# A residual stream turned by VectorE in place of TensorE, and weight sums kept split: one planned fp32 layer on one core

## The chip, the cores and the metric

One core of a Trainium2 chip runs the whole layer. The metric is the device time of the run in microseconds (us). TensorE (PE) multiplies, VectorE (DVE) and ScalarE (ACT) do elementwise work, SyncE (SP) issues nearly all transfers between DRAM and on-chip memory, and 16 DMA engines carry them out. Each engine takes its own instructions in the order in which they were emitted, and waits where an operand or a buffer is not ready.

## The reference

The layer has 1024 tokens of width D = 1024 and an FFN of width FF = 3072, all float32:

```python
h = rms_norm(x, norm1_w)
q, k, v, g_ret, x_lru, y_lru, gate_ret, gate_lru = split(h @ w_in)
# A: 4 heads of chunked retention with decay, rotary, group norm, swish gate, @ w_ret_o
# B: causal conv (4), block-diagonal gates, linear recurrence, GeLU branch, @ w_lru_o
x1 = x + (sigmoid(gate_ret) * A + sigmoid(gate_lru) * B) @ w_out
h2 = rms_norm(x1, norm2_w)
g, u = split(h2 @ ffn_w_up)
x2 = x1 + (gelu(causal_conv(g, 3)) * u) @ ffn_w_down
out = rms_norm(x2, norm_f_w)
rms_norm(y, w) = y * rsqrt(mean(y * y, -1) + 1e-6) * w
```

## The kernel before, in words

**Products.** Operands of a product are float32, split in two parts (hi, a cast on ACT, L772; lo = source − hi on DVE, L773), and multiplied in three passes (hi·hi, lo·hi, hi·lo). A job of `mm_fast` makes 256 output columns for all 1024 tokens by the seven products of the Winograd form of Strassen's method: `prod` issues 12 matmuls of 128x512 each (L899), 84 for a job. The weight side needs sums of blocks, S1 to S4 (DVE, L817 to L824), the activation side T1 to T4. The third part of a group is called `wl`, `wrr` or `wsr` where it is lo of a weight, `h…`, `b…` and `t…` are activations, `g` a bank of PSUM.

**Stages.** Times of the profiled execution: values of the heads first (to 95 us); 20 jobs on w_in, with the retention heads and the recurrent blocks as side work between their matmuls (to about 597); 4 jobs each on w_ret_o and w_lru_o (to about 800); 4 jobs on w_out, `out_job(n)`, which make x1 (to about 880); 24 FFN-up jobs (to about 1338); 12 FFN-down jobs in three groups (to 1566); and a tail.

**Order.** The Python code records every operation with its buffers, and a planner (`Prog`) orders them by a table of costs (DMA landing, engine time), with a seed and a jitter for its search. What stands under `within(slack, side)` may be placed later than its place in the code by some slack; `side` work on PE fits between the main matmuls. Any change of operations or of a constant gives a new order everywhere.

**x1 in the kernel before.** A pair n of out_job makes channel blocks 2n and 2n+1: `x1q` holds x by channel (128 channels x 1024 tokens for each block), and L1620 adds the product to it. For n < 3 `turn2` then turns it to token order on PE (128x128 transposes against the identity `cst`, L1680, into a bank `a`), ACT copies the bank to `x1k` (L1686), SP stores x1k to x1_d (by token; `x_d` in the profile), and ACT squares x1k with a sum over channels (L1692) into `nst`. L1642 multiplies x1q by norm2_w in place, `h2_steps` (L1596 to L1605) makes the T sums. For n = 3 the turns come after the jobs, and the scaled values go to a buffer of their own, `x1w` (L1645). The reciprocal root for every token goes to DRAM and comes back on all partitions as `rowt` (L1083); the outputs of FFN up are multiplied by it (L1415). FFN down reads x1_d by token, adds the product (L1813), squares (L1818), takes the root (L1822), multiplies by norm_f_w in place (L1827), scales (L1837 on ACT, L1839 on DVE) and stores (L1840).

**Weight sums ahead of time.** `presum` (L1024 to L1038) makes S1 to S4 for four units of w_out (w0 to w3) and two of w_up (u0, u1), stores them in DRAM (`ss_d`), and their jobs load them (`wr<-ss_d`) and split them. The first presum starts when job 8 of w_in is done, and one follows every second job.

**Retention heads.** Each head's output is turned (L1392), stored to `ot_d`, gathered again as `oc`, and multiplied into its buffers by eight DVE steps (L1406). The convolution of the recurrent branch is a row of DVE steps (L1260).

Of the kernel before, what the change touches and what calls it, by code (L numbers as in the profile page):

```python
# [263 lines left out]
class Prog:  # L264
# [59 lines left out]
    def cost(self, o, how, n, outs, ins, args, kw):  # L324
# [321 lines left out]
    SEED, JITTER, ROUNDS, STALL, URGE = 6, 400.0, 7, 150.0, 6000.0  # L646
# [11 lines left out]
    def emit(self, engines, make, behind):  # L658
        at, sent = {}, []
        for o in self.order:  # L660
# [34 lines left out]
UNS = 1  # L695
# [11 lines left out]
TSLACK = 8000.0  # L707
TEARLY = 6000.0
RELOAD = 0
RNORM = 0  # L710
X1K = 1
HALVES = 0
LATE2 = 2
SQSLACK = 40000.0
PRE = (0, 0, 4, 2)
PRE_AT = 8
PRE_STEP = 2
# [14 lines left out]
def record(prog, fx):  # L732
# [3 lines left out]
    row_d, og_d, u_d, y_d, sg_d, t1_d, x1_d, td_d, to_d, ff_d, rot_d, ss_d, v_d, kt_d, ot_d = (  # L736
        fx[n + "_d"] for n in ("row", "og", "u", "y", "sg", "t1", "x1", "td", "to", "ff", "rot", "ss", "v", "kt", "ot"))
# [38 lines left out]
    def blocks(jb):  # L776
# [17 lines left out]
        def block(nm):  # L794
# [9 lines left out]
            elif jb.pres is not None:  # L804
                if nm == "A22":
                    t = get("wf")
                    SY.dma_start(t, cut(jb.src(1), 1))
                    blk[nm] = *split(t, "w", True), 0
                else:
                    i = int(nm[1])  # L810
                    t = get("wr", FLAT)
                    SY.dma_start(t, jb.pres[i // 2])
                    both(nm, f"S{i + 1}", t, True)
# [210 lines left out]
    def presum(src, dst):  # L1024
# [7 lines left out]
        SY.dma_start(dst[0], s)  # L1032
# [527 lines left out]
    V.memset(rcol, 0.0)  # L1560
    S.activation(st[:, 0:1], st[:, 1:2], AF.Sqrt)
# [22 lines left out]
    x1q, x1w, x1k = {}, [], {}  # L1584
# [26 lines left out]
    def out_job(n):  # L1611
# [3 lines left out]
        def emit(m, h, src, d, sign):  # L1615
            if m not in seen:
                seen.add(m)
                SY.dma_start(q[:, m], xt[:, 2 * n + m].rearrange("h p c -> p h c"))
            t = q[:, m] if h is None else q[:, m, h]
            (V.tensor_add if sign > 0 else V.tensor_sub)(t, t, src)  # L1620
            if n == 3 and HALVES:
                if len(x1w) < 4:
                    x1w.append(get("x1w", QUAD))
                S.activation(x1w[3][:, m, h], t, AF.Copy, scale=pc("norm2_w", 2 * n + m))

        def done(m, d):
            ch = 2 * n + m
            if n == 3 and HALVES:
                if m == 1:
                    next(h2steps)  # L1630
                return
            if UNU:
                if m == 0:
                    x1w.append(get("x1w", QUAD) if n == 3 else q)
                if n < 3:
                    if m == 1:
                        with within(TEARLY, True):
                            for t in range(0, 8, 2):
                                turn2(t, 2 * n, n)
                        with within(TEARLY + 2000.0):  # L1640
                            for i in range(2):
                                S.activation(q[:, i], q[:, i], AF.Copy, scale=pc("norm2_w", 2 * n + i))  # L1642
                            next(h2steps)
                    return
                S.activation(x1w[n][:, m], q[:, m], AF.Copy, scale=pc("norm2_w", ch))  # L1645
                if m == 1:
                    next(h2steps)
            elif UNS:
                hi, lo = scaled_split(q[:, m], pc("norm2_w", ch), "h")
                for h in range(2):  # L1650
                    h2u[f"B{ch // 4 + 1}{h + 1}", ch % 4] = hi[:, h], lo[:, h]

        def post():
            if UNU:
                return None
            if n == 1:
                return turns(0, 4, 0)
            if n == 2:
                return turns(4, 2, 1)

        return Job(pair_src(w_out, n), mop, emit, done, post, fast=n < 4 - STD_W, js=(0, 1, 3, 2), shape=PAIR,
                   pres=pre_of.get(("w", n)))

    def turn(t, ch0, nch, part):
        ps = bank("a")
        for i in range(nch):
            src = x1q[(ch0 + i) // 2][:, (ch0 + i) % 2, t // 4]
            PE.transpose(ps[:, 128 * i:128 * i + 128], src[:, 128 * (t % 4):128 * (t % 4) + 128], ident)
        o = get("x1s")
        S.copy(o[:, :128 * nch], ps[:, :128 * nch])  # L1670
        SY.dma_start(x1_d[128 * t:128 * t + 128, 128 * ch0:128 * ch0 + 128 * nch], o[:, :128 * nch])
        S.activation(ps[:, :128 * nch], ps[:, :128 * nch], AF.Square, accum_out=nst[:, part, t:t + 1])

    def turn2(t, ch0, part):
        ps = bank("a")
        for k in range(2):
            c = 128 * ((t + k) % 4)
            for i in range(2):
                src = x1q[(ch0 + i) // 2][:, (ch0 + i) % 2, t // 4]
                PE.transpose(ps[:, 256 * k + 128 * i:256 * k + 128 * i + 128], src[:, c:c + 128], ident)  # L1680
        if X1K:
            odd = part % 2
            if not odd:
                x1k[t] = get("x1k", PAIR)
            o = x1k[t]
            S.copy(o[:, :, 256 * odd:256 * odd + 256], ps.rearrange("p (k c) -> p k c", k=2))  # L1686
            if odd:
                SY.dma_start(x1_d[128 * t:128 * t + 256, 128 * ch0 - 256:128 * ch0 + 256].rearrange(
                    "(k p) c -> p k c", k=2), o)
                with within(SQSLACK, True):  # L1690
                    for k in range(2):
                        S.activation(o[:, k], o[:, k], AF.Square, accum_out=nst[:, part // 2, t + k:t + k + 1])  # L1692
            return
        o = get("x1s")
        S.copy(o, ps)
        for k in range(2):
            b = slice(256 * k, 256 * k + 256)
            SY.dma_start(x1_d[128 * (t + k):128 * (t + k) + 128, 128 * ch0:128 * ch0 + 256], o[:, b])
            if RELOAD:
                continue  # L1700
            S.activation(ps[:, b], ps[:, b], AF.Square, accum_out=nst[:, part, t + k:t + k + 1])

    def turns(ch0, nch, part):
        for t in range(8):
            turn(t, ch0, nch, part)
            yield 0.9
# [7 lines left out]
    for h in range(2):  # L1714
        for t in range(4 * h, 4 * h + 4, 2 if UNU else 1):
            with within(TSLACK, True):
                if UNU:
                    turn2(t, 6, 3)
                    for i in range(t, t + 2 if RELOAD else t):
                        b = get("xs", FLAT)  # L1720
                        SY.dma_start(b, x1_d[128 * i:128 * i + 128, :])
                        S.activation(b, b, AF.Square, accum_out=nst[:, 0, i:i + 1])
                else:
                    turn(t, 6, 2, 2)
        with within(TSLACK, True):
            a, b, c, e = (nst[:, i, 4 * h:4 * h + 4] for i in range(4))
            v, r = nst[:, 5, 4 * h:4 * h + 4], nst[:, 4, 4 * h:4 * h + 4]
            if not RELOAD:
                V.tensor_add(v, a, b)
            if not RELOAD and not X1K:  # L1730
                V.tensor_add(v, v, c)
            if UNU and not RELOAD and not X1K:
                V.tensor_add(v, v, e)
            V.tensor_scalar(v, a if RELOAD else v, 1.0 / D, EPS, ALU.mult, ALU.add)
            rstd_of(r, v, a)
    rows_of(nst[:, 4, :], True, 1)
    if UNU:
        pass
    elif UNS:
        for k in (0, 1, 4, 5, 2, 3, 6, 7):  # L1740
            rescale(x1q, k, "norm2_w")
        operand(h2, of_quads(x1q), ("B11", "B21", "B22"), False)
    else:
        for h in range(2):
            for k in range(KT):
                t = x1q[k // 2][:, k % 2, h]
# [205 lines left out]
```

## Time and profile before

| | |
|---|---|
| time, median of 3 runs | 1575.1 us (1574.51 to 1575.68) |
| profiled execution, its own time | 1574.89 us |
| its span, first to last instruction | 1573.1 us |
| PE busy | 1563.2 us, 99% |
| DVE busy | 1278.3 us, 81% |
| ACT busy | 883.9 us, 56% |
| granted TensorE clock | 0.999 |
| share of the 16 DMA engines | 56% |

A row of the groups reads: line, engine, operation, output and inputs by name, shape, count | busy time, mean ns of one | idle time of the engine just before them, and what ended it. Matmuls are pipelined, so the durations of neighbours overlap; the distance from start to start is what a matmul takes of the engine's time. A row of the windows gives the stretch and its length, then busy time of PE, its weight loads, DVE, ACT and POOL with the number of instructions that began there, the granted clock, the share of the DMA engines, and GB/s. A row of the DMA issues ends with the median time from issue to landing. A row of the chain of waits gives start, length, and the engine and line that the chain ran through.

### The profile page before, as it was taken

The page shows a single profiled execution, that of the slowest core. Times are in us where ns is not written, and L with a number is a line of the kernel's source. Part 1 is how long each engine was busy: PE and PEld are TensorE (multiplying, and loading weights), DVE is VectorE, ACT ScalarE, POOL GpSimd, SP SyncE. Part 2 cuts the span into 40 slices and gives each one's busy share as a digit, 9 for nine tenths or more (in the row PEclk, how much of TensorE's full clock was granted, in tenths as well). Part 3 has the DMA queues.
Part 4 walks back from the last instruction along what each step waited for, and adds up shares of the span by engine and source line. Part 5 has one row for each costly group of instructions (what it writes and reads, how often), then busy time and mean ns, then how long its engine had stood idle before and what let it go on. Part 6 is the DMA issues. An engine that isn't in the chain of part 4 may idle for free.

```text
span 1573.1 us, 19066 instructions
## 1 busy us (share of the span) xinstructions
PE 1563.2 (99%) x6956; PEld 1295.1 (82%) x6956; DVE 1278.3 (81%) x1712; ACT 883.9 (56%) x1181; POOL 0.2 (0%) x4
## 2 busy tenths in 40 slices
PE   9999999999999999999999999999999999999998
PEld 8888888888878888888888888888888888888886
DVE  5996876988888979978795987788888778977795
ACT  7464567577468568645447854444444445554463
POOL 0000000000000000000000000000000000000000
PEclk9999999999999999999999999999999999999999
DMA  9424354457397579968354522465666335786751
GB/s 333 153 71 150 101 160 147 124 198 261 104 317 261 174 235 349 346 212 336 107 201 151 171 94 70 154 198 185 195 194 219 111 95 194 278 285 249 260 217 67
DMA packets 145150, 303.96 MB, mean 193 GB/s; under 512 B 11168, under 2 KB 60448, under 8 KB 145056
## 3 DMA queue, kind: packets, MB, share of 16 engines
q1 hardware_dynamic: 144624, 302.21, 56.2%
q8 instruction: 55, 0.90, 0.2%
q10 hardware_dynamic: 432, 0.53, 0.1%
q14 instruction: 39, 0.32, 0.1%
HBM read 209.36 MB, written 93.33 MB: 192 GB/s over the span
## 4 chain that ended last, share of the span: by engine, by line
PE 96%; DMA 2%; DVE 1%; ACT 1%; issue 0%; SPq 0%; DVEq 0%; ACTq 0%
PE g L899 84%; PE g L1499 6%; PE a L1273 2%; PE a L1362 1%; PE a L1369 1%; PE a L1361 1%; DMA wgr<-w_gate 1%; PE a L1355 0%; DMA bf<-og_d 0%; PE a L1680 0%; DMA oc<-ot_d 0%; DMA kl<-kt_d 0%; DMA xq<-xt 0%; DVE bf L1017 0%; DVE wrr L773 0%
## 5 line engine op out<-in xcount | busy, mean ns | idle before, releaser
L899 PE MATMUL g<-bh,wh 128*128 128x512 f32 x1728 | 676.2, 391 | 0.0
L899 PEld LDWEIGHTS g<-bh,wh 128*128 128x128 f32 x1728 | 324.5, 188 | 66.2 <-ACT g L920 0.4
L899 PE MATMUL g<-bh,wl 128*128 128x512 f32 x880 | 345.7, 393 | 0.0
L899 PE MATMUL g<-bl,wh 128*128 128x512 f32 x864 | 338.7, 392 | 0.0
L899 PE MATMUL g<-bh,wrr 128*128 128x512 f32 x824 | 321.5, 390 | 0.0
L772 ACT CAST wh<-wr 128x1024 fp32r<-128x1024 f32 (+1 forms) x220 | 198.4, 919 | 71.0 <-DVE wr L824 20.1
L899 PEld LDWEIGHTS g<-bh,wl 128*128 128x128 f32 x880 | 165.2, 188 | 33.9
L899 PEld LDWEIGHTS g<-bl,wh 128*128 128x128 f32 x864 | 162.3, 188 | 33.1
L899 PEld LDWEIGHTS g<-bh,wrr 128*128 128x128 f32 x824 | 154.7, 188 | 32.0
L773 DVE TENSOR_TENSOR wrr<-wr,wh 128x1024 fp32r<-128x1024 f32 (+1 forms) x154 | 152.4, 992 | 35.2 <-ACT wh L772 35.1
L899 PE MATMUL g<-tdr,wh 128*128 128x512 f32 x320 | 124.5, 389 | 0.0
L772 ACT CAST wh<-ws 128x1024 fp32r<-128x1024 f32 x66 | 69.5, 1053 | 81.8 <-DVE ws L818 41.9
L899 PE MATMUL g<-hl,wh 128*128 128x512 f32 x288 | 112.1, 389 | 0.0
L899 PE MATMUL g<-hh,wh 128*128 128x512 f32 x288 | 112.1, 389 | 0.0
L911 DVE TENSOR_TENSOR ub<-ub,g 128x512 f32<-128x512 f32 x72 | 49.4, 686 | 66.1 <-PE g L899 65.9
L773 DVE TENSOR_TENSOR wl<-wr,wh 128x1024 fp32r<-128x1024 f32 x66 | 80.5, 1219 | 8.1 <-ACT wh L772 2.7
L773 DVE TENSOR_TENSOR wl<-ws,wh 128x1024 fp32r<-128x1024 f32 x66 | 80.5, 1220 | 6.0 <-PE g L899 3.9
L906 ACT ACTIVATE ub<-g 128x512 f32<-128x512 f32 x72 | 42.9, 596 | 71.0 <-PE g L899 68.5
L899 PE MATMUL g<-tsr,wh 128*128 128x512 f32 x208 | 81.0, 390 | 0.0
L920 ACT ACTIVATE g<-g 128x512 f32<-128x512 f32 x72 | 41.9, 583 | 55.7 <-PE g L899 55.5
L911 DVE TENSOR_TENSOR ua<-ua,g 128x512 f32<-128x512 f32 x72 | 49.3, 684 | 28.5 <-PE g L899 27.3
L899 PEld LDWEIGHTS g<-tdr,wh 128*128 128x128 f32 x320 | 60.1, 188 | 12.5
(268 smaller groups left out, 2527.0 us busy)
## 6 DMA issues: line engine op xcount, KB each, us to landing
wr<-w_up SPq DMA_DIRECT2D x50, 512.0 KB, 4.5
wr<-w_in SPq DMA_DIRECT2D x48, 512.0 KB, 5.2
dw<-w_dn SPq DMA_DIRECT2D x42, 512.0 KB, 5.7
ff_d<-gc SPq DMA_DIRECT2D x24, 512.0 KB, 3.4
wr<-ff_d SPq DMA_DIRECT2D x24, 512.0 KB, 9.2
td<-td_d SPq DMA_DIRECT2D x24, 512.0 KB, 6.9
x<-x_d SPq DMA_DIRECT2D x24, 512.0 KB, 10.0
td_d<-dw SPq DMA_DIRECT2D x18, 512.0 KB, 6.0
```

Source lines behind the costliest of these rows:

```text
L772: S.copy(hi, src)
L773: V.tensor_sub(lo, src, hi.bitcast(F32))
L899: PE.matmul(ps, (hi, lo)[a][:, c], o[b], start=first and n == 0, stop=n == 11, skip_group_check=True)
L906: S.activation(cut(d[m], h), ps, AF.Copy, scale=scale)
L911: (V.tensor_sub if m else V.tensor_add)(u, u, ps)
L920: S.activation(Y, X, AF.Copy)
L1273: PE.matmul(ps, wg[a][:, g, cs], xs[b][:, k], start=q == 0, stop=q == 5)
L1361: PE.matmul(p2[:, 0:256], q[:, bs], rst[cur], start=True, stop=False)
L1362: PE.matmul(p2[:, 0:256], s, v, start=first, stop=True)
L1369: made.append(PE.matmul(p3[:, 0:256], kd[h][:, bs], v, start=True, stop=True))
L1499: PE.matmul(ps[t], a[i][:, 128 * t:128 * t + 128], b[j], start=k == 0 and i + j == 0, stop=k == KT - 1 and i == 1)
```

## The change

x1 leaves each half of an out job by channel: the half of 128x512 goes to a new DRAM buffer `xb_d`, its square is summed over the channel blocks in `x1s` (a square on ACT, an addition on DVE; the first block of each half squares straight into x1s), and norm2_w multiplies it half by half, in place for n < 3. At the start of FFN up eight fp32 matmuls with `x1s` as the stationary operand and a column of ones sum over the partitions, one result column for 128 tokens. The token order is made during FFN-up jobs 5 to 12: a load of 128 tokens from xb_d (pieces of 512 bytes), one DVE transpose in 32x32 blocks, four stores to x1_d. Since DVE turns only blocks of 32, the channels of x, of the rows of w_in and w_up, the columns of w_out and the norm weights are laid out in another order by the host. The sums of w2, w3, u0 and u1 are split at once and stored as two parts, loaded into `wh` and `wr`, and need no cast and no subtraction later. Presums start after job 4, one at each job. The last norm multiplies into a buffer of its own, `fin`. The planner's cost of an fp32 matmul has a floor, its seed is 4 in place of 6, and options that were off are gone. The 6448 fp32r matmuls are the same.

```diff
-                o.occ, o.lat = 4 * n / 2.4 + 5, 4 * n / 2.4 + 220
+                o.occ, o.lat = max(4 * n / 2.4 + 5, 108), max(4 * n / 2.4, 110) + 220
...
-    SEED, JITTER, ROUNDS, STALL, URGE = 6, 400.0, 7, 150.0, 6000.0
+    SEED, JITTER, ROUNDS, STALL, URGE = 4, 400.0, 7, 150.0, 6000.0
...
+PRE = (0, 0, 4, 2)
+HALVED = ("w2", "w3", "u0", "u1")
...
+TURN0, TURNSLACK = 5, 20000.0
...
-PRE_AT = 8
-PRE_STEP = 2
+PRE_AT = 4
+PRE_STEP = 1
...
-                    SY.dma_start(t, jb.pres[i // 2])
-                    both(nm, f"S{i + 1}", t, True)
+                    p, done = jb.pres
+                    if done:
+                        v, t = get("wh", FLAT, F32R), get("wr", FLAT, F32R)
+                        SY.dma_start(v.bitcast(F32), p[i // 2, 0])
+                        SY.dma_start(t.bitcast(F32), p[i // 2, 1])
+                        for c, n in ((0, nm), (TH, f"S{i + 1}")):
+                            blk[n] = v, t, c
+                    else:
+                        t = get("wr", FLAT)
+                        SY.dma_start(t, p[i // 2, 0])
+                        both(nm, f"S{i + 1}", t, True)
...
+            if halved:
+                hi, lo = split(t, "w", True)
+                SY.dma_start(to[0], hi.bitcast(F32))
+                SY.dma_start(to[1], lo.bitcast(F32))
...
             (V.tensor_add if sign > 0 else V.tensor_sub)(t, t, src)
...
+            with within(TEARLY, True):
+                SY.dma_start(xb_d[k, :, TH * h:TH * h + TH], t)
+                acc = x1s[0][:, h]
+                z = get("x1z") if h in x1s[1:] else acc
+                S.activation(z, t, AF.Square)
+                if h in x1s[1:]:
+                    V.tensor_add(acc, acc, z)
+                x1s.append(h)
+            with within(TEARLY + 2000.0):
+                S.activation(x1w[n][:, m, h], t, AF.Copy, scale=pc("norm2_w", k))
...
-                            for t in range(0, 8, 2):
-                                turn2(t, 2 * n, n)
...
-                PE.transpose(ps[:, 256 * k + 128 * i:256 * k + 128 * i + 128], src[:, c:c + 128], ident)
...
+    def turn(t):
+        a, b = get("x1t", FLAT), get("x1r", FLAT)
+        SY.dma_start(a.rearrange("p (k i) -> p k i", k=KT), xb_d[:, :, P * t:P * t + P].rearrange("k p i -> p k i"))
+        V.transpose(b.view(lambda z: z.rearrange("p (c k j) -> p k c j", c=4, k=KT), FLAT[1]),
+                    a.view(lambda z: z.rearrange("p (k c i) -> p k c i", k=KT, c=4), FLAT[1]))
+        for i in range(4):
+            SY.dma_start(x1_d[P * t:P * t + P, 256 * i:256 * i + 256].rearrange("(c i) r -> i c r", c=4),
+                         b[32 * i:32 * i + 32].rearrange("i (c r) -> i c r", c=4))
...
+        for t in range(8):
+            PE.matmul(ps[:, t:t + 1], x1s[0][:, t // 4, P * (t % 4):P * (t % 4) + P], fx["ones"], start=True, stop=True)
+        V.tensor_scalar(v, ps, 1.0 / D, EPS, ALU.mult, ALU.add)
+        rstd_of(r, v, a)
...
+            if TURN0 <= i < TURN0 + 8:
+                with within(TURNSLACK, True):
+                    turn(i - TURN0)
...
-            V.tensor_mul(cut(d, h), cut(d, h), cut(nf, h))
+            if m not in fin:
+                fin[m] = get("fin", FLAT)
+            V.tensor_mul(cut(fin[m], h), cut(d, h), cut(nf, h))
...
+    perm = ar(D).reshape(4, KT, 32).transpose(1, 0, 2).ravel()
```

Three places of the order. In the changed file the lines are a few higher or lower: the main matmul is L905 there, the cast L770, the subtraction L771, the gathered head's step L1423, the convolution's L1277.

TensorE where FFN up begins (`g` is the PSUM bank of a product, `wh`, `wrr`, `wfr`, `wr` the weights, `a` the bank of the small results). Before:

```order
L899 MATMUL g_7083<-bh_6751,wfr_7110 128x512
L899 MATMUL g_7265<-hh_6869,wh_7217 128x512
L899 MATMUL g_7265<-hl_6880,wh_7217 128x512
L1680 MATMUL a_7206<-cst,x1q_7129 128x128 x3
L1680 MATMUL a_7208<-cst,x1q_7129 128x128 x3
L899 MATMUL g_7265<-hh_6869,wrr_7271 128x512
L899 MATMUL g_7265<-hh_6869,wh_7217 128x512
L899 MATMUL g_7265<-hl_6880,wh_7217 128x512
```

and now:

```order
L905 MATMUL g_7319<-bl_6968,wh_7174 128x512
L905 MATMUL g_7319<-bh_6956,wr_7178 128x512
L905 MATMUL g_7319<-bh_7029,wh_7174 128x512
L1681 MATMUL a_7337<-ones,x1s_6807 128x1 x8
L905 MATMUL g_7319<-bl_7066,wh_7174 128x512
L905 MATMUL g_7319<-bh_7029,wr_7178 128x512
```

The transposes of the last pair stood two matmuls behind the first product of FFN up; no transposes stand there now, and the eight ones matmuls stand 30 main matmuls behind the first of FFN up.

ScalarE during the out jobs. Before:

```order
L1686 COPY x1k_6826<-a_6765 128x2x256
L1686 COPY x1k_6830<-a_6767 128x2x256
L1686 COPY x1k_6844<-a_6833 128x2x256
L1642 ACTIVATE x1q_6552<-x1q_6552,par 128x1024 x2
L1686 COPY x1k_6863<-a_6840 128x2x256
L772 CAST hh_6869<-x1q_6552 128x1024
```

and now, at a later pair:

```order
L1648 ACTIVATE x1z_7101<-x1q_6810 128x512
L1648 ACTIVATE x1z_7115<-x1q_6810 128x512
L926 ACTIVATE g_7126<-g_7088 128x512
L1653 ACTIVATE x1q_6810<-x1q_6810,par 128x512
L770 CAST hh_7141<-x1q_6810 128x1024
L912 ACTIVATE ub_7149<-g_7113 128x512
L770 CAST bh_7154<-ts_6943 128x1024
L1653 ACTIVATE x1q_6810<-x1q_6810,par 128x512
```

The copies of banks are gone; squares stand ahead of the scalings, and each scaling of a half (L1653) stands directly ahead of the cast that makes an operand of it.

VectorE at the end of the second retention head. Before:

```order
L1406 SCALAR_TENSOR_TENSOR ua_2335<-oc_2752,par,ua_2335 128x8x32
L1406 SCALAR_TENSOR_TENSOR ub_2317<-oc_2770,par,ub_2317 128x8x32
L1406 SCALAR_TENSOR_TENSOR ua_2335<-oc_2752,par,ua_2335 128x8x32
L1406 SCALAR_TENSOR_TENSOR ub_2317<-oc_2770,par,ub_2317 128x8x32 x2
L911 TENSOR_TENSOR ub_2749<-ub_2749,g_2702 128x512
L773 TENSOR_TENSOR wl_2867<-wr_2677,wh_2755 128x1024
L773 TENSOR_TENSOR wl_2877<-ws_2773,wh_2794 128x1024
```

and now:

```order
L1423 SCALAR_TENSOR_TENSOR ub_2385<-oc_2871,par,ub_2385 128x8x32
L917 TENSOR_TENSOR ua_2841<-ua_2841,g_2793 128x512
L1423 SCALAR_TENSOR_TENSOR ub_2385<-oc_2871,par,ub_2385 128x8x32
L1423 SCALAR_TENSOR_TENSOR ua_2391<-oc_2854,par,ua_2391 128x8x32
L1423 SCALAR_TENSOR_TENSOR ub_2385<-oc_2871,par,ub_2385 128x8x32
L1277 SCALAR_TENSOR_TENSOR xc_2866<-ub_2537,par,xc_2866 128x1023
L771 TENSOR_TENSOR wl_2952<-ws_2837,wh_2888 128x1024
```

A convolution step now stands between the last scalings of the gathered head and the remainder `wl` that the next product needs; the addition `L917` stands between the scalings and no longer behind them.

More of the change, by code (lines that the diff above doesn't have):

```diff
@@ L694 @@
 STD_LO = 0
-UNS = 1
 LEAD = 3
@@ L735, in record @@
     rst, bst, mv, rs = fx["rst"], fx["bst"], fx["mv"], fx["rs"]
-    row_d, og_d, u_d, y_d, sg_d, t1_d, x1_d, td_d, to_d, ff_d, rot_d, ss_d, v_d, kt_d, ot_d = (
-        fx[n + "_d"] for n in ("row", "og", "u", "y", "sg", "t1", "x1", "td", "to", "ff", "rot", "ss", "v", "kt", "ot"))
+    row_d, og_d, u_d, y_d, sg_d, t1_d, x1_d, xb_d, td_d, to_d, ff_d, rot_d, ss_d, v_d, kt_d, ot_d = (
+        fx[n + "_d"] for n in ("row", "og", "u", "y", "sg", "t1", "x1", "xb", "td", "to", "ff", "rot", "ss", "v", "kt", "ot"))
     x, positions, normf, w_in, w_v, w_ro, w_lo, w_out, w_up, w_dn, w_gate, out, xt = (
@@ L1560, in record @@
     V.memset(rcol, 0.0)
+    V.memset(fx["ones"], 1.0)
     S.activation(st[:, 0:1], st[:, 1:2], AF.Sqrt)
@@ L1583, in record @@
     h2, h2u = {}, {}
-    x1q, x1w, x1k = {}, [], {}
+    x1q, x1w, x1s = {}, [], []
     def h2_steps():
@@ L1615, in emit @@
         def emit(m, h, src, d, sign):
+            k = 2 * n + m
+            if not x1s:
+                x1s.append(get("x1s", PAIR))
+            if not seen:
+                x1w.append(get("x1w", QUAD) if n == 3 else q)
             if m not in seen:
                 seen.add(m)
-                SY.dma_start(q[:, m], xt[:, 2 * n + m].rearrange("h p c -> p h c"))
-            t = q[:, m] if h is None else q[:, m, h]
+                SY.dma_start(q[:, m], xt[:, k].rearrange("h p c -> p h c"))
@@ L1626, in done @@
+            with within(TEARLY + 2000.0):
+                S.activation(x1w[n][:, m, h], t, AF.Copy, scale=pc("norm2_w", k))
         def done(m, d):
-            ch = 2 * n + m
-            if n == 3 and HALVES:
-                if m == 1:
+            if m == 1:
+                with within(TEARLY + 2000.0):
                     next(h2steps)
[L1631 to L1637, printed above, removed]
-                            for t in range(0, 8, 2):
-                                turn2(t, 2 * n, n)
[L1640 to L1661, printed above, removed]
-                   pres=pre_of.get(("w", n)))
[L1664 to L1706, printed above, removed]
+        return Job(pair_src(w_out, n), mop, emit, done, fast=n < 4 - STD_W, js=(0, 1, 3, 2), shape=PAIR,
+                   pres=pre_of.get(("w", n)))
+    def turn(t):
[6 more added lines that the diff above has]
+                         b[32 * i:32 * i + 32].rearrange("i (c r) -> i c r", c=4))
@@ L1713, in record @@
     drain()
[L1714 to L1735, printed above, removed]
-    rows_of(nst[:, 4, :], True, 1)
[L1737 to L1746, printed above, removed]
-                V.scalar_tensor_tensor(t, t, pc("norm2_w", k), cut(row[0], h), ALU.mult, ALU.mult)
-                if k % 2:
-                    put(h2, f"B{k // 4 + 1}{h + 1}", k % 4 // 2, split(x1q[k // 2][:, :, h, :], "h"))
+    with within(TSLACK, True):
+        a, r, v, ps = nst[:, 0, 0:8], nst[:, 4, 0:8], nst[:, 5, 0:8], bank("a")[:, 0:8]
+        for t in range(8):
+            PE.matmul(ps[:, t:t + 1], x1s[0][:, t // 4, P * (t % 4):P * (t % 4) + P], fx["ones"], start=True, stop=True)
+        V.tensor_scalar(v, ps, 1.0 / D, EPS, ALU.mult, ALU.add)
+        rstd_of(r, v, a)
+    rows_of(nst[:, 4, :], True, 1)
     def post_ff(i, gv):
@@ L1768, in down_of @@
         return fetch
-    if not UNU:
-        tsets(h2, of_quads(x1q))
     def emit_row(m, h, src, d, sign):
@@ L1786, in post @@
                 return sums_of(down_of(g), td_d[g], jp)
-        plain = UNS and i < STD_U and not UNU
+        plain = False
         return Job(pair_src(w_up, i), h2u if plain else h2, emit_row if plain else emit_as(),
@@ L1799, in down_job @@
     def down_job(g, t):
-        x1, fin = {}, set()
+        x1, fin = {}, {}
         def fetch(m):
@@ L1834, in done @@
             for c in (m, 1 - m):
-                o, to = cut(d, c), out[rows(t, m), TH * c:TH * c + TH]
+                o, to = cut(fin[m], c), out[rows(t, m), TH * c:TH * c + TH]
                 if c == m:
```

45 lines of the change are left out of this document (23 added, 22 removed).

## The prediction

> **What bounds the kernel now.** I read the page's busy lines first, then its chain that ended last, then busy time stage by stage, then the pieces of the chain around the edited code.
>
> ```profile
> span 1573.1 us, 19066 instructions
> PE 1563.2 (99%) x6956; PEld 1295.1 (82%) x6956; DVE 1278.3 (81%) x1712; ACT 883.9 (56%) x1181; POOL 0.2 (0%) x4
> PE 96%; DMA 2%; DVE 1%; ACT 1%; issue 0%; SPq 0%; DVEq 0%; ACTq 0%
> ```
>
> TensorE is busy 99% of the span and is 96% of the chain, so a change shows only by the TensorE work that it adds or removes, or by a wait that it makes or ends. The stages, with the columns start:end, length, then busy time of PE, its weight loads, DVE and ACT:
>
> ```profile
> 0.00:95.00 95.00, 93.69 (x414) 78.10 (x415) 73.96 (x123) 55.31 (x80) 0.20 (x4) 1.00 0.58 203
> 160.00:280.00 120.00, 120.00 (x541) 99.98 (x540) 92.38 (x144) 79.50 (x107) 0.00 (x0) 1.00 0.44 137
> 280.00:440.00 160.00, 160.00 (x726) 133.63 (x725) 138.02 (x237) 98.96 (x136) 0.00 (x0) 1.00 0.56 183
> 450.00:597.00 147.00, 146.11 (x651) 120.32 (x650) 126.88 (x185) 98.63 (x131) 0.00 (x0) 1.00 0.71 245
> 817.00:885.00 68.00, 67.41 (x328) 55.65 (x327) 49.67 (x56) 46.59 (x68) 0.00 (x0) 1.00 0.49 160
> 885.00:1330.00 445.00, 445.00 (x1964) 368.44 (x1964) 362.92 (x400) 216.05 (x287) 0.00 (x0) 1.00 0.47 151
> ```
>
> PE idles 1.31 us in the first stage, which the change leaves alone, 0.89 us at the last retention heads (450 to 597), 0.59 us where the out jobs end (817 to 885), and nowhere in FFN up. The granted clock is 1.00 throughout.
>
> **The change part by part.**
>
> *The 64 transposes leave TensorE.* The chain has them as pieces (start, us, count); two of the fourteen groups and what ends the stage:
>
> ```profile
> 824.44 0.66 PE a L1680 x6
> 825.10 0.92 PE g L899 x4
> 826.02 0.87 PE a L1680 x8
> ...
> 877.86 0.57 issue
> 878.43 1.23 DVE wrr L773
> ...
> 884.55 0.44 PE a L1680 x4
> 884.99 680.97 PE g L899 x3004
> ```
>
> 0.66/6, 0.87/8 and 0.44/4 all give 0.109 us, so 64 cost 7.0 us of the path; the last row gives a plain matmul's share, 680.97/3004 = 0.2267 us, the ruler for the gaps below. The groups view shows longer durations:
>
> ```profile
> L1680 PE MATMUL a<-cst,x1q 128*128 128x128 f32 x64 | 9.3, 272 | 0.3 <-DVE x1q L1620 0.3
> L1680 PEld LDWEIGHTS a<-cst,x1q 128*128 128x128 f32 x64 | 7.7, 140 | 2.3 <-DVE x1q L1620 0.7
> L1355 PE MATMUL a<-ua,ub 128*128 128x128 f32 x64 | 11.8, 273 | 0.0
> L1355 PEld LDWEIGHTS a<-ua,ub 128*128 128x128 f32 x64 | 11.5, 189 | 2.3
> ```
>
> The 272 ns overlap the neighbour's; the chain's spacing counts. **−7.0 us.** The Trainium skill (TensorE: Matmul & The Clock Gate, Part 4: PE-mode transpose) gives about 275 ns for such a transpose inside a kernel. The 272 ns row agrees as a duration; as a cost on the path the chain's 0.109 us contradicts it, and I go by the chain.
>
> *Eight one-column matmuls come.* An fp32 matmul is two passes (L1355 has 64 for 32 products), so 16 passes, each with its 128x128 weights. No row has one output column. Below, they cannot cost less than nothing, since they add work to TensorE; above, if no weight load is hidden, 16 x 0.189 = 3.0 us. The nearest row is the same fp32 weight form with 128 columns, spaced 0.109 us like the transposes, and their own 140 ns loads fitted in that spacing: 16 x 0.109 = **+1.75 us**. By the Trainium skill (same page, Back-to-back issue gap: up to 64 columns about 25 ns) an estimate is 16 x 0.025 = 0.4 us, and the sum would be 1.35 us lower. No row of this trace tests that.
>
> *The boundary of out and up.* The 0.59 us idle here is two waits, both at the last out pair:
>
> ```profile
> PE a L1273 <- ACT li L1275: 0.7, 1, 0.7
> PE a L1680 <- DVE x1q L1620: 0.3, 1, 0.3
> PE g L899 <- DVE wrr L773: 0.3, 1, 0.3
> ```
>
> The transposes waited for the last residual addition, and the weight remainder stood behind that addition on DVE. In the new order nothing on PE waits for that addition at once: the ones matmuls stand 30 matmuls after the first up matmul, 31 x 0.2267 = 7.0 us, while the square and the addition to x1s that they need end about 6.1 us after it (a sum over the DVE and ACT rows ahead at 0.69, 1.22 and 0.63 us). A margin of 0.9 us; and the weight sums of the first up unit come already split there, without a DVE step. **−0.6 us.** PE takes its instructions in order: if the margin goes, the ones matmuls wait, and all up matmuls behind them are late by as much.
>
> *DVE and ACT in the out stage.* What leaves and what comes:
>
> ```profile
> L1686 ACT COPY x1k<-a 128x512 f32<-128x512 f32 x16 | 9.1, 587 | 12.7 <-PE a L1680 12.7
> L1692 ACT ACTIVATE x1k<-x1k 128x512 f32<-128x512 f32 x16 | 9.9, 631 | 0.2 <-DMA x_d<-x1k 0.2
> L1642 ACT ACTIVATE x1q<-x1q,par 128x1024 f32<-128x1024 f32 x6 | 6.6, 1152 | 0.0
> L1620 DVE TENSOR_TENSOR x1q<-x1q,g 128x512 f32<-128x512 f32 x8 | 5.5, 684 | 5.5 <-PE g L899 5.5
> L773 DVE TENSOR_TENSOR wl<-ws,wh 128x1024 fp32r<-128x1024 f32 x66 | 80.5, 1220 | 6.0 <-PE g L899 3.9
> 1568.91 0.72 ACT ub L1837
> ```
>
> ACT loses 16 x 0.587 + 16 x 0.631 + 8 x 1.152 (six and two more for the last pair) = 28.7 us and gets 16 scalings of half size at 0.72 (the last row, same form) and 16 squares at 0.63 = 21.6: lighter by 7. DVE gets 14 additions x 0.684 = 9.6 us on top of 49.67 of 68, and loses the subtractions of two out units and two up units, 8 x 1.22 = 9.8, part of them here. Both stay far below 68: **0**, hidden by the matmuls. If that cover went, the DVE part would cost 9.6 us at most.
>
> *A new wait.* For the first three pairs the scaling overwrites x1q in place, so ACT's L1653 of the new kernel waits until the store of the same half to xb_d has landed. Stores of this size and of twice it in rows of this trace:
>
> ```profile
> x_d<-x1k SPq DMA_DIRECT2D x8, 512.0 KB, 4.6
> bf<-og_d SPq DMA_DIRECT2D x14, 512.0 KB, 8.2
> v_d<-v SPq DMA_DIRECT2D x16, 256.0 KB, 2.4
> ```
>
> In the new order the tightest scaling comes 17 matmuls = 3.85 us behind its store, with 1.8 us more until PE needs what follows it. At 2.4 us ACT does not wait; queued behind ACT's scaling are the casts of the activations that PE multiplies next. **0**, bounded above by the slowest row, 8.2 us: 8.2 − 3.85 − 1.8 = 2.55 us for each of six channel blocks, 15.3 us.
>
> *Eight VectorE transposes in FFN up, and x1_d by 32 stores.*
>
> ```profile
> L1392 DVE STREAM_TRANSPOSE ox<-ob 128x1024 f32<-128x1024 f32 x8 | 9.9, 1236 | 0.2
> x<-x_d SPq DMA_DIRECT2D x24, 512.0 KB, 10.0
> ```
>
> 8 x 1.24 = 9.9 us into the 82 us that DVE has free between 885 and 1330. Their loads are issued 15 to 44 matmuls (3.4 to 10 us) ahead, so a load of 10.0 us would hold DVE for up to 6.6 us. The first weights split behind any of them are used at least 68 matmuls later, 15.4 us: **0**. x1_d is read only in FFN down. The SP queue is passed by 64 more transfers; in the out stage the engines' DMA share is 0.49.
>
> *Weight sums earlier, and stored split.* Six units' sums (4 additions each, 24 x 0.68 = 16.3 us of DVE) move from 312 to 552 us to about 170 to 335, with the 9.8 us of subtractions of the split ones. DVE has 27.6 us free in 160 to 280 and 22.0 in 280 to 440. So the room suffices by a little: (92.38 + 138.02 x 55/160 + 26.1 less the 2.7 of the one unit that is there now) / 175 = 93%: **0**, with rival B as the price of it going wrong.
>
> *The tail.* Today the last Square is followed by a scaling on ACT, and the root after it starts late:
>
> ```profile
> 1567.24 0.19 ACT L1818 ACTIVATION_READ_ACCUMULATOR a<-ub 128x1 f32 x1
> 1567.34 0.71 ACT L1837 ACTIVATE ua<-ua,nst 128x512 f32<-128x512 f32 x1
> 1567.95 0.28 ACT L1822 ACTIVATE nst<-nst 128x1 f32<-128x1 f32 x1
> ```
>
> In the new order the root stands right behind the Square (0.5 us won) and the last addition behind one more DVE scaling (about 0.35 lost): **−0.15 us**.
>
> *Sum.* 1573.1 − 7.0 + 1.75 − 0.6 − 0.15 = 1567.1 us span. The profiled execution took 1574.89, 1.8 more than its span: 1568.9; the median of the runs is 1575.1, 0.2 above it: **1569.1 us**, 0.4% less. Layout, buffer and planner constants cost nothing of themselves; the order they lead to is what was read.
>
> **The rivals.** A measurement of this kernel tells about 0.2% (3.15 us) from no change.
>
> *B: a new PE wait at the second head's end.* The order puts eight scalings of the gathered head at about 334 us ahead of the remainder wl that PE needs next. Prices, and what DVE did at such a place before:
>
> ```profile
> L1406 DVE SCALAR_TENSOR_TENSOR ua<-oc,par,ua 128x256 f32<-128x256 f32 x16 | 7.7, 480 | 2.2 <-DMA oc<-ot_d 2.1
> L1260 DVE SCALAR_TENSOR_TENSOR xc<-ua,par,xc 128x1023 f32<-128x1023 f32 x4 | 5.1, 1282 | 2.7 <-ACT xc L1256 2.7
> 446.88 0.48 DVE L1406 SCALAR_TENSOR_TENSOR ub<-oc,par,ub 128x256 f32<-128x256 f32 x1 [1.49 <-DMA oc<-ot_d]
> ```
>
> Behind a late oc load stand five scalings, one addition, one convolution step and the subtraction itself: 5 x 0.40 + 0.60 + 1.28 + 1.22, with their starts some 5.6 us, against three matmuls (0.7 us) on PE in the same stretch of the order: 4.9 us, hence 1574.0, no change. For it: the 1.49 us wait for oc above, and the crowded DVE. Against it: at 446.88 the same pile of 7 us made no PE wait, since DVE ran ahead of the order by then.
>
> *G: the small terms all go well.* The 0.89 us at the last heads goes with the sums moved out of there, and the one-column passes cost a share near their column's: 1569.1 − 0.9 − 1.35 = 1566.9. For it: the idle time lies where presums stood. Against it: its largest piece, 0.7, waits for ACT li, which a load precedes.
>
> *C: the in-place scaling waits for its store.* The mechanism above: from a landing of 3.85 + 1.8 = 5.65 us on ACT holds PE, at 8.2 us by 15.3 us in all: 1584.4, slower (slower by 0.2% from some 7.2 us). Against it: stores of 256 KB take 2.4 us.
>
> *D: each transpose costs its whole 272 ns.* Then 64 x 0.272 = 17.4 us leave, 10.4 more: 1558.7. Against it: the chain's rows lie end to end at 0.109.
>
> That the change does not do what it says is excluded by the order: the transposes' rows are gone from PE and nothing but the eight ones rows came.
>
> **How the numbers follow.** Forecast A 0.63, B 0.18, G 0.13, C 0.04, D 0.02. A's own range, from the ends of the one-column passes (0 to 3.0) and stalls of a microsecond either way, is 1566.3 to 1571.4. The range 1565.5 to 1573.0 holds A, G and the half of B with a smaller wait; C, D and the other half, 0.15, are left out. Faster by more than 0.2% means below 1571.9: A but for 0.02 (0.61), G, D and a fifth of B (0.04) = 0.80. Same: the rest of A and B = 0.16. Slower: C = 0.04.
>
> **What would show it.** Right: PE's busy time down by about 5.3 us in 817 to 890, no L1680 group, a group of 16 ones passes spaced about 0.11 us apart, no PE idle at the boundary, the last matmul ending about 6 us earlier. Wrong: in the waits of PE, a row ending in DVE wl or ACT wh near 200, 334 or 446 us (B); ACT idle until DMA xb_d ahead of L1653 (C); ones rows 0.19 us apart; DVE idle until DMA x1t with PE waiting after it.

## The result and the profile after

The changed kernel takes 1567.12 us (median of 6 runs, 1566.76 to 1568.2) against 1575.34 (6 runs, 1574.51 to 1576.17): 0.9948 of the time before, 95% interval 0.9936 to 0.9961, so 8.2 us faster. Its profiled execution took 1568.2 us with a span of 1566.4; a later one (e5) 1567.54 with 1565.7. First the page's span, busy times and chain of the changed kernel:

```profile
span 1566.4 us, 19108 instructions
PE 1556.1 (99%) x6908; PEld 1289.9 (82%) x6908; DVE 1294.6 (83%) x1727; ACT 879.1 (56%) x1158; POOL 0.2 (0%) x4
PE 98%; DMA 1%; DVE 0%; ACT 0%; issue 0%; SPq 0%; ACTq 0%; DVEq 0%
```

TensorE (PE) is still 99% busy, with 7.1 us less to do (1563.2 before); DVE does 16 us more in a shorter span, and it did not matter. The stages, with the columns as before:

```profile
0.00:95.00 95.00, 92.46 (x413) 77.12 (x414) 73.28 (x119) 55.71 (x79) 0.20 (x4) 1.00 0.57 203
160.00:280.00 120.00, 120.00 (x540) 99.94 (x539) 100.44 (x159) 77.26 (x104) 0.00 (x0) 1.00 0.59 199
280.00:440.00 160.00, 160.00 (x725) 133.43 (x725) 140.74 (x240) 103.02 (x142) 0.00 (x0) 1.00 0.58 190
450.00:597.00 147.00, 146.16 (x653) 120.85 (x652) 125.73 (x180) 106.20 (x137) 0.00 (x0) 1.00 0.61 210
817.00:888.00 71.00, 71.00 (x322) 59.03 (x321) 59.23 (x73) 44.83 (x64) 0.00 (x0) 1.00 0.66 244
888.00:1330.00 442.00, 442.00 (x1951) 365.80 (x1950) 365.72 (x395) 207.58 (x265) 0.00 (x0) 1.00 0.53 173
```

From 817 to 888 PE no longer idles at all. At the last heads (450 to 597) it idles 0.84 us, as before (0.89), though at another place. In the first stage, whose work did not change, it idles 2.54 us here; in e5, the same kernel in the same order, 1.35. So a microsecond of difference between two executions comes from the start alone, and a comparison of two single traces is good to about that. What the chain shows where FFN up begins, and the waits of PE in the whole trace:

```profile
875.89 3.17 PE g L905 x14
879.07 1.68 PE a L1681 x16
880.74 9.46 PE g L905 x41
```

```profile
PE g L1516 <- ACT hh L1104: 1.5, 1, 1.5
PE g L1574 <- DVE sc L1571: 1.0, 1, 1.0
PE a L1379 <- DVE state L1390: 0.8, 1, 0.8
```

The 16 passes of the eight ones matmuls cost 1.68 us, 0.105 each. No wait for x1 is left; of the three waits two belong to the start and one (0.8) to a retention head.

Where the time went, by start-to-start distances on PE between 815 and 890 us, less 0.2267 us for every main matmul there: 8.51 us were left before (64 transposes, their switches and waits, beside 293 main matmuls) and 1.87 now (16 passes beside 322). That is −6.64 of the −6.7 us between the two spans. The tail, from the last matmul's start to the end, is 0.25 us shorter; by start-to-start distances the first stage lost 0.3, and the heads kept what they had, give or take.

### The profile page after: what moved, and what is told of

Same layout as the page of the kernel before. It is cut to its first block, busy times and chain, and to the rows that moved or that the text cites. A ratio compares the mean times of both kernels' runs of the same rounds, so it can differ in the third digit from the quotient of the medians.

```text
span 1566.4 us, 19108 instructions
## 1 busy us (share of the span) xinstructions
PE 1556.1 (99%) x6908; PEld 1289.9 (82%) x6908; DVE 1294.6 (83%) x1727; ACT 879.1 (56%) x1158; POOL 0.2 (0%) x4
## 4 chain that ended last, share of the span: by engine, by line
PE 98%; DMA 1%; DVE 0%; ACT 0%; issue 0%; SPq 0%; ACTq 0%; DVEq 0%
PE g L905 87%; PE g L1516 6%; PE a L1290 3%; PE a L1379 1%; PE a L1378 1%; PE a L1386 1%; PE a L1372 0%; DMA xq<-xt 0%; DMA wr<-w_in 0%; DMA to_d<-bf 0%; PE a L1681 0%; ACT a L1752 0%; ACT fin L1773 0%; DVE ua L917 0%; PE g L1521 0%; DVE wrr L771 0%
## 5 line engine op out<-in xcount | busy, mean ns | idle before, releaser
L905 PE MATMUL g<-bh,wh 128*128 128x512 f32 x1728 | 676.2, 391 | 0.0
L905 PEld LDWEIGHTS g<-bh,wh 128*128 128x128 f32 x1728 | 324.4, 188 | 66.8 <-ACT g L926 0.3
L905 PE MATMUL g<-bh,wl 128*128 128x512 f32 x880 | 344.1, 391 | 0.0
L905 PE MATMUL g<-bl,wh 128*128 128x512 f32 x864 | 339.0, 392 | 0.0
L905 PE MATMUL g<-bh,wrr 128*128 128x512 f32 x768 | 299.5, 390 | 0.0
L770 ACT CAST wh<-wr 128x1024 fp32r<-128x1024 f32 (+1 forms) x216 | 195.1, 916 | 75.3 <-PE g L905 21.1
L905 PEld LDWEIGHTS g<-bh,wl 128*128 128x128 f32 x880 | 165.2, 188 | 34.6 <-DVE wl L771 0.7
L905 PEld LDWEIGHTS g<-bl,wh 128*128 128x128 f32 x864 | 162.3, 188 | 33.1
L771 DVE TENSOR_TENSOR wrr<-wr,wh 128x1024 fp32r<-128x1024 f32 (+1 forms) x150 | 147.5, 984 | 33.1 <-ACT wh L770 32.9
L905 PEld LDWEIGHTS g<-bh,wrr 128*128 128x128 f32 x768 | 144.2, 188 | 29.9
L770 ACT CAST wh<-ws 128x1024 fp32r<-128x1024 f32 x70 | 73.7, 1052 | 94.1 <-DVE ws L824 54.6
L905 PE MATMUL g<-tdr,wh 128*128 128x512 f32 x320 | 124.5, 389 | 0.0
L905 PE MATMUL g<-hh,wh 128*128 128x512 f32 x288 | 112.0, 389 | 0.0
L905 PE MATMUL g<-hl,wh 128*128 128x512 f32 x288 | 112.0, 389 | 0.0
L917 DVE TENSOR_TENSOR ub<-ub,g 128x512 f32<-128x512 f32 x72 | 49.3, 685 | 54.7 <-PE g L905 46.5
L771 DVE TENSOR_TENSOR wl<-wr,wh 128x1024 fp32r<-128x1024 f32 x66 | 80.4, 1218 | 12.0 <-PE g L905 6.1
L771 DVE TENSOR_TENSOR wl<-ws,wh 128x1024 fp32r<-128x1024 f32 x66 | 80.5, 1219 | 8.5 <-PE g L905 5.5
L905 PE MATMUL g<-tsr,wh 128*128 128x512 f32 x208 | 81.0, 389 | 0.0
L917 DVE TENSOR_TENSOR ua<-ua,g 128x512 f32<-128x512 f32 x72 | 49.3, 684 | 34.4 <-PE g L905 33.6
L912 ACT ACTIVATE ua<-g 128x512 f32<-128x512 f32 x72 | 43.0, 597 | 60.6 <-PE g L905 56.8
```

What stands on the lines that cost most here:

```text
L770: S.copy(hi, src)
L771: V.tensor_sub(lo, src, hi.bitcast(F32))
L905: PE.matmul(ps, (hi, lo)[a][:, c], o[b], start=first and n == 0, stop=n == 11, skip_group_check=True)
L912: S.activation(cut(d[m], h), ps, AF.Copy, scale=scale)
L917: (V.tensor_sub if m else V.tensor_add)(u, u, ps)
```

## The experiments

All ratios are to the kernel before, run beside it on the same chip. e1 to e4, e5 to e8 and e9 to e12 shared a chip each.

**e1, 64 transposes put back**, of a constant tile, planned with the rest:

```diff
+    def spin(n):
+        for t in range(0, 8, 2):
+            ps = bank("a")
+            for k in range(4):
+                PE.transpose(ps[:, 128 * k:128 * k + 128], ident, ident)
...
             if m == 1:
+                if n < 3:
+                    with within(TEARLY, True):
+                        spin(n)
...
+        spin(3)
         a, r, v, ps = nst[:, 0, 0:8], nst[:, 4, 0:8], nst[:, 5, 0:8], bank("a")[:, 0:8]
```

> The changed kernel (1567.1 us) with 64 transposes of 128x128 put back on TensorE, in the same places of the out jobs but of a constant tile into a bank that nobody reads, so that they bring no ACT copy, no store and no wait for x1. Theory (the gain is the transposes' issue time, 0.109 us each): +7.0 us, 1574.1, so nearly the time of the kernel before. Rival D (a transpose costs its whole 272 ns row): +17.4, 1584.5. Rival plan (the gain comes from a luckier order and fewer waits; the transposes were hidden): within 1.5 us of 1567.1.

Measured: 1576.77 us, 1.0013 (1.0004 to 1.0022), about 10 us above the changed kernel. More than the theory's 7.0, far less than 17.4, and not the time of the changed kernel, as a mere gain of a luckier order would have it. The trace shows why it decides nothing finer: the planner moved the free transposes about (some to 262 us, 25 in a row at 406) and gave a new order with waits of its own, such as these two.

```profile
PE g L905 <- DVE wl L771: 0.6, 1, 0.6
PE a L1290 <- DVE xsl L771: 0.4, 1, 0.4
```

So e7 repeats it with the order held.

**e7, the same 64 transposes in the changed kernel's own order**, emitted after the planning directly ahead of the ones matmuls (`mark` holds the bank of the ones matmuls and the identity, and in e12 also `xb_d`):

```diff
+            if o.eng == "PE" and o.args[0].base is self.mark[0].base and not sent_extra:
+                sent_extra.append(1)
+                for j in range(64):
+                    real.transpose(self.mark[0][:, 128 + 128 * (j % 3):256 + 128 * (j % 3)].ap(), self.mark[1].ap(), self.mark[1].ap())
             inst = at[o.line](getattr(real, o.how), args, kw)
```

> The changed kernel in exactly its own order, with 64 transposes of a constant tile emitted in one row directly ahead of the ones matmuls, after the planning, so that nothing else moves. Theory (0.109 us each): +7.0 us over the changed kernel. Rival D (272 ns each): +17.4. If such a row of small work lowers the granted clock as the 64 passes of one column did (it fell from 1.00 to 0.5 after 3.8 us of them): 3.8 us at 0.109 and then 29 at 0.213, +10 us, and some slow matmuls behind it.

Measured: 1573.48 us, 0.9995 (0.9986 to 1.0004); the changed kernel beside it 1566.61 (e5). The difference is 6.9 us, 0.107 for each. The chain of e7 (L674 are the added transposes, L1687 the ones matmuls):

```profile
877.94 6.99 PE a L674 x64
884.93 1.68 PE a L1687 x16
886.61 676.05 PE g L909 x2981
```

6.99/64 = 0.109 us, to the third digit what the chain of the kernel before had. Rival D is out: a transpose shows as 272 ns in the groups, and its removal saves 109. The row of 7 us did not lower the clock either:

```profile
880.00:884.00 4.00, 4.00 (x39) 4.00 (x37) 2.53 (x3) 0.00 (x0) 0.00 (x0) 1.00 0.08 33
884.00:888.00 4.00, 4.00 (x32) 3.74 (x31) 0.17 (x1) 0.10 (x1) 0.00 (x0) 1.00 0.00 0
```

**e2, the ones matmuls four times over**, all in one row:

```diff
-        for t in range(8):
+        for t in (*range(8),) * 4:
             PE.matmul(ps[:, t:t + 1], x1s[0][:, t // 4, P * (t % 4):P * (t % 4) + P], fx["ones"], start=True, stop=True)
```

> The changed kernel with the eight one-column fp32 matmuls made four times over, 48 more passes. Theory (spaced as in the trace of the changed kernel, 1.68 us for 16): +5.0 us, 1572.1. By the weight loads' own 0.19 us each, none hidden: +9.1, 1576.2. By the issue floor of one column that the skill's page states (25 ns): +1.2, 1568.3.

Measured: 1576.58 us, 1.0013 (1.0004 to 1.0022): about 10 us above the changed kernel for 48 more passes. By the numbers alone the second expectation (9.1, weight loads unhidden) would be taken. The trace says otherwise. The chain, and then the windows (the column ahead of the last two is the granted clock):

```profile
878.47 9.97 PE a L1681 x64
888.43 21.57 PE g L905 x86
```

```profile
879.00:881.00 2.00, 2.00 (x20) 2.00 (x20) 2.00 (x3) 0.90 (x2) 0.00 (x0) 1.00 0.69 259
881.00:885.00 4.00, 4.00 (x26) 4.00 (x25) 2.12 (x2) 0.00 (x0) 0.00 (x0) 0.65 0.02 10
885.00:890.00 5.00, 5.00 (x21) 4.71 (x21) 0.17 (x1) 0.90 (x2) 0.00 (x0) 0.50 0.00 0
890.00:893.00 3.00, 3.00 (x9) 2.33 (x9) 2.33 (x4) 2.13 (x3) 0.00 (x0) 0.60 0.00 0
893.00:900.00 7.00, 7.00 (x32) 5.76 (x31) 4.47 (x12) 3.71 (x6) 0.00 (x0) 1.00 0.09 31
```

The passes start 0.112 us apart for the first 3.8 us, then 0.213 apart, and the clock stands at 0.50; it is back only some 4 us after the row, so that the first plain matmuls are slow too. A wait for weights would be there from the first passes on.

**e8, the same 64 passes in four groups of 16**, with 24 plain matmuls between, in the changed kernel's own order. The sums of those plain matmuls are not used (they repeat the operands of the last main matmul, `last`), and the extra work is 48 passes and 72 matmuls of 504 columns:

```diff
...
+            if o.eng == "PE" and o.args[0].base is self.mark[0].base:
+                for _ in range(3):
+                    at[o.line](getattr(real, o.how), args, kw)
+                sent_extra.append(1)
+                if len(sent_extra) in (2, 4, 6):
+                    for _ in range(24):
+                        real.matmul(self.mark[0][:, 8:512].ap(), last[0][1], last[0][2][:, 0:504], start=True, stop=True, skip_group_check=True)
```

> The changed kernel in its own order, with the eight ones matmuls made four times over as before, but in four groups of 16 passes with 24 plain matmuls of 504 columns between them. Theory (the passes cost 0.112 us, and the second half of them was slow only because a long row of one-column work lowered the granted clock): all 64 passes spaced by 0.11 us, clock 1.00 throughout, 7.2 us for them in all. Rival (the passes themselves get slow after some number of them, or the clock falls by their number and not by the length of the row): spacing 0.21 us in the later groups, and the clock below 1.

```profile
878.34 1.68 PE a L1693 x16
880.02 5.58 PE a L681 x24
885.60 1.68 PE a L1693 x16
887.28 5.55 PE a L681 x24
892.83 1.68 PE a L1693 x16
894.50 5.55 PE a L681 x24
900.05 1.68 PE a L1693 x16
```

```profile
885.00:890.00 5.00, 5.00 (x32) 4.45 (x31) 0.00 (x0) 0.00 (x0) 0.00 (x0) 1.00 0.00 0
890.00:895.00 5.00, 5.00 (x32) 4.46 (x31) 0.00 (x0) 0.00 (x0) 0.00 (x0) 1.00 0.01 3
```

Every group costs 1.68 us, 6.7 in all against 9.97 in one row, and the clock stays at 1.00 (one run, 1589.12 us, which holds the plain matmuls too). So the loss of e2 is the length of the row, not the number of passes. The theory's price for the change's own 16 passes holds.

**e3 and e6, the way of x1 alone**: the weight sums as before.

```diff
-HALVED = ("w2", "w3", "u0", "u1")
+HALVED = ()
-PRE_AT = 4
-PRE_STEP = 1
+PRE_AT = 8
+PRE_STEP = 2
```

> The changed kernel with the weight sums as before: none kept split, first presum after job 8 and one at every second job. What is left is the way of x1. Theory (the sums' change is hidden and worth nothing): 1567.1 within 1.5 us, the scatter of a new order. Rival (the earlier, split sums gave a part of the gain, since the idle time at 440 to 480 us went with them): 1568.6 to 1571, with PE waiting again between 440 and 600 us.

> The kernel with only the way of x1 changed (weight sums as before) once more, beside the changed kernel on one chip. Theory (the sums are worth nothing): within 1.5 us of the changed kernel. Its earlier trace has 1.1 us less of waiting on TensorE than the changed kernel's, so if that holds it is 1 us faster. Rival (the split sums gave a part of the gain): 1.5 us or more slower.

Measured: 1567.54 (0.9957, 0.9944 to 0.9969) and 1567.63 (0.9954, 0.9941 to 0.9966). e5, the changed kernel itself beside e6:

> The changed kernel itself, beside the next ones on the same chip, as their base: ratio 0.9948 to the kernel before, as in its first runs (0.9936 to 0.9961).

gave 1566.61 (0.9949, 0.9935 to 0.9962). The difference of 1.0 us lies inside both intervals, and the spans of e5 and e6 (1565.7 and 1565.4) stand the other way round. The expectation of e6 that the way of x1 alone would be 1 us faster, by its shorter waits, did not hold. The sums bring at most about a microsecond; the way of x1 alone makes the gain.

**e4, e9, e10, e11, the planner's seed.** Each is one of the two kernels with nothing but the seed changed; e4's edit, and the others likewise:

```diff
-    SEED, JITTER, ROUNDS, STALL, URGE = 4, 400.0, 7, 150.0, 6000.0
+    SEED, JITTER, ROUNDS, STALL, URGE = 6, 400.0, 7, 150.0, 6000.0
```

> The changed kernel with the planner's seed of the kernel before (6). Only the order differs. Theory (the seed is worth the idle of PE at a few places, 1 us or so): 1566.1 to 1568.6. Rival (the order of seed 4 was picked and other orders lose several us at a retention head's end): 1570 or more, with a PE wait of 2 us or more in one place.

> The kernel before with the planner's seed of the change (4). Only the order differs. Theory (the change is worth 5.2 us of TensorE's issue time whatever the order; a seed moves the waits by a few us): 1574 to 1579, so that at seed 4 the change is worth 7 to 12 and at seed 6 (e4) 3.5. Rival (seed 4 is the better order for either kernel, and part of the 8.2 us is the seed): 1570 to 1573.

> The kernel before with a third seed (5). Theory: 1574 to 1579, by the waits that its order has. With seeds 4 and 6 it gives a mean over orders of the kernel before.

> The changed kernel with the same third seed. Theory: 1567 to 1571 (between seed 4 and seed 6), and the mean over the three seeds 5 to 6 us below the mean of the kernel before. Rival (the gain is the choice of a lucky order): the means differ by 3 us or less.

| seed | kernel before | changed kernel |
|---|---|---|
| 4 | 1575.68, 1.0003 (0.9994 to 1.0013) | 1566.61, 0.9949 (0.9935 to 0.9962), the change as it is |
| 5 | 1577.58, 1.0018 (1.0008 to 1.0027) | 1571.46, 0.998 (0.9971 to 0.9989) |
| 6 | 1, as it was | 1570.89, 0.9976 (0.9967 to 0.9985) |

The mean of the three ratios is 1.0007 before and 0.9968 after: 0.0039, or 6.1 us. By medians on one chip the change is worth 3.5 us at seed 6 (1574.42 to 1570.89) and 6.1 at seed 5, by the ratios 8.5 at seed 4. The two orders of the changed kernel that were slower lose it mostly ahead of the out jobs, so not by the way of x1: of seed 6's 3.7 us of PE waits behind the start, 3.3 lie there. Seed 6, the longest of its PE waits, and seed 5, its chain at ret_o with a window of it:

```profile
PE g L905 <- ACT ua L912: 1.2, 2, 0.7
PE g L1574 <- DVE sc L1571: 1.0, 1, 1.0
PE g L905 <- DVE ub L917: 0.9, 1, 0.9
PE g L905 <- DVE wl L771: 0.8, 1, 0.8
```

```profile
613.99 1.23 DVE ds L1017
615.22 1.14 DVE li L1306
616.35 0.60 DVE wrr L771
616.96 1.13 DVE li L1308
618.09 1.15 DVE wrr L771
619.28 30.92 PE g L905 x128
620.00:623.00 3.00, 3.00 (x9) 2.31 (x8) 1.60 (x2) 1.55 (x2) 0.00 (x0) 0.50 1.04 392
```

In the second, DVE works off the last recurrent block and two weight remainders; PE goes on until 617.7 us and then stands still for 1.6. Behind that the granted clock is 0.50, and the next matmuls start 0.43 us apart in place of 0.227: the 128 of the last chain row take 1.9 us more than at 0.2267. So the wait cost about 2 us, and the clock about as much again. The kernel before at seed 5 instead waits at the place that the change removes:

```profile
PE a L1680 <- ACT x1k L1686: 1.6, 1, 1.6
PE a L1680 <- DVE x1q L1620: 0.8, 1, 0.8
```

So the rival of e11 (all of it luck) falls: the difference of the means is 6, not 3 or less. The rival of e9 falls too: seed 4 is no better for the kernel before. But the expectations of e4 and e11 missed as well: a seed is worth 4 us in the changed kernel, not one, and seed 5 came out 0.5 us above the range given. Seed 4, the change's own, is the best of the three for it, so by this mean some 2 of the 8.2 us are the choice of that order. Whether the earlier sums have a part in the waits of the slower orders was not tested.

**e12, each store to xb_d four times**, in the changed kernel's own order:

```diff
             inst = at[o.line](getattr(real, o.how), args, kw)
+            if o.how == "dma_start" and getattr(o.args[0], "base", None) is self.mark[2]:
+                for _ in range(3):
+                    at[o.line](getattr(real, o.how), args, kw)
```

> The changed kernel in its own order, with each store of a half of x1 to xb_d issued four times, so that the in-place scaling waits for the last of them. In the changed kernel's trace these stores take 6.3 us, and ACT idles 2.7 us for them with no wait on TensorE. Rival C as predicted (ACT holds TensorE from a landing of 5.65 us on, six times): with landings of 9 us or more, 20 us or more, 1587. Theory (ACT has more room than that): some ACT waits, and up to 2 us on TensorE, 1567 to 1569.

Measured: 1654.64 us, 1.0506 (1.049 to 1.0521), 88 us above the changed kernel, far beyond either expectation. The chain and the waits of ACT:

```profile
815.49 2.00 DMA xb_d<-x1q
817.50 2.00 DMA xb_d<-x1q
819.52 1.99 DMA xb_d<-x1q
```

```profile
ACT x1q L1656 <- DMA xb_d<-x1q: 69.6, 11, 11.2
```

The four stores write the same place, and SP waited for each to land, 2.0 us or more, before it issued the next: 48 waits, 106.5 us in all, which held up the queue with all that is behind it. Thus the edit blocked two things, ACT's scaling and the queue; the granted clock fell too (0.54 to 0.93 in the windows of 20 us from 820 to 980). It tells nothing of their shares, nor of the landing from which a late store alone would stop PE. It gives one number: a store of 256 KB with nothing else issued beside it lands in 2.0 us.

None of these versions beats the changed kernel beyond the uncertainty.

## Why the prediction was right

It forecast 1569.1 us, faster, and the cause: TensorE's issue time. By its steps:

- **The transposes, −7.0.** Right, and shown by itself: 6.99 us in e7's chain, 6.9 by its time. The forecast hung on reading the chain's 0.109 us and not the group's 272 ns.
- **The ones matmuls, +1.75.** 1.68 in the chain. The 25 ns of the Trainium skill (TensorE: Matmul & The Clock Gate, Back-to-back issue gap) stand there as the gap of matmuls taken by themselves, which the page says leaves out the weight loads. Every pass here has a load of its own, and the passes are 0.112 us apart, as are their weight loads.
- **The boundary, −0.6.** Undersized; this is the term that was off. I took the 0.59 us in which PE was not busy. But a busy time of overlapping matmuls covers the start of a gap: the chain quoted in the prediction has 0.57 + 1.23 us from 877.86 to 879.70, in which PE issued six transposes (0.65), and by start-to-start distances the two waits cost 1.08. All of it is gone. With the switches at the 14 groups, the stage gave 6.64 where the steps summed to 5.85. The margin of the ones matmuls held: the last addition to x1s ended at 877.98 us, and they start at 878.90.
- **DVE and ACT in the out stage, 0.** Right: DVE is at 59.23 of 71 us there, and PE does not idle.
- **The in-place scaling, 0.** The zero is right, its reason was not: ACT did wait for stores.

```profile
xb_d<-x1q SPq DMA_DIRECT2D x16, 256.0 KB, 6.3
ACT x1q L1653 <- DMA xb_d<-x1q: 2.7, 2, 1.9
```

  The 6.3 us are the median of the five stores whose landing is on record: 2.0, 2.0, 6.3, 7.2 and 8.5 us, the last two of the last pair, which does not scale in place. The two that ACT waited for were the first two of the stage, and they landed after 2.5 and 4.6 us. ACT had run ahead of the order: it stood at the first scaling 0.6 us behind the store, where I had counted 3.85, and so waited 1.9 us and then 0.8, with no wait on PE behind either. The store of 6.3 us, past the 5.65 from which rival C was to decide, had its scaling 7.2 us later and was not waited for. So C's case did not arise. My price of 2.4 us was itself a median of four stores, 2.1 to 5.4 us; landings spread more than I allowed for.
- **DVE's transposes and the sums, 0.** Right. The transposes take 1239 ns, as predicted from L1392, and DVE never waited for their loads (4.4 us to landing). With the earlier sums DVE is busy 152.65 of the 175 us from 160 to 335, 87%, less than the 93% feared.
- **Rival B** did not come at its place. The eight scalings stood at 333.6 to 338.4 us as the order said, with 0.8 us of waiting for oc, and PE went on without a wait. That PE can lose by what DVE and ACT have in front of them is real all the same: in other orders (e4, e11) such waits, at other places, take back about 4 and 5 us.
- **The tail, −0.15.** −0.25.
- **Rival G** named 1566.9, nearer to the measured time than the forecast, but neither of its terms came: the heads still idle 0.84 us, and the passes cost 1.68. That its number fits is chance.
- **One sign was ill-chosen.** PE's busy time in 817 to 890 did not fall by 5.3 us; it rose from 72.41 to 73.00. An engine that never idles fills a fixed window with the work that comes next. The fall shows in the busy time of the whole span (7.1 us) and in the distances. The other signs came, the last matmul 6.5 us earlier among them.

The rest of the 2.0 us between 1569.1 and 1567.1: the sum of the steps gave a span of 1567.1, and the two traces of the changed kernel have 1566.4 and 1565.7, with executions 1.1 and 0.9 us above their groups' medians, where the one before stood 0.2 below. So by the first trace 0.7 us of the 2.0 are the span, and 1.3 the step from one profiled execution to the median. The start of the program, where PE idles 1.35 to 2.54 us in the same order, makes some of that; what else separates a profiled execution from the median stays open.

## What to carry to other kernels

Price work on a saturated engine by its start-to-start distance in the chain, not by the duration of its rows, and price a gap in the same way, since busy time hides the part that overlaps. Where a planner or scheduler reorders everything after an edit, measure an edit also with the order held (e7) and over a few seeds (6.1 us over three here, 3.5 to 8.5 singly); one seed of each kernel mixes the edit with its luck. And do not take an operand's landing time from a median of another stage: stores of the same 256 KB took from 2.0 to 8.5 us within this one.

## What the runs showed of the hardware

A long row of one-column fp32 matmuls lowers the granted clock although TensorE is busy all the time: in e2 from 1.00 to 0.50 after 3.8 us (34 passes), for about 10 us, the plain matmuls behind it included, at a cost of about 5 us. Groups of 16 passes (1.7 us) between plain matmuls do not (e8), and neither do 64 transposes in a row of 7.0 us (e7), which are as densely issued but have 128 columns. The transposes differ in more than that (a constant tile, one pass each), so that the single column makes the difference is likely and not separated.

A wait can lower the clock too: 1.6 us in which TensorE stood still were followed by 0.50 in e11, and by 1.00 in e10, where the wait ended at 884.7 us. By the clock records of the traces the stretches at 0.50 ahead of the tail last 3.41 us (e11), 10.24 (e2) and 6.83, 10.24 and 23.89 (e12), all multiples of 3.41. The Trainium skill (TensorE: Matmul & The Clock Gate, Part 1: The HAM clock gate) ties the clock to how busy the array has been in a window of about 3.4 us; the 3.8 us and these lengths agree with such a window. If that is the rule, one-column work counts as little or nothing in it; e2 suggests this and no run shows it by itself. The eight matmuls of this change do not lower the clock (1.00 from 817 to 1330); four times as many in one row would have cost the whole gain.
